# Own semaphores, an early close of the Tile context and one last wait in a split GELU-multiply kernel

## The chip, the cores and the metric

One core of one Trainium2 chip. The metric is the device time of one execution in microseconds (us), as the median over executions. Each listed execution has also a *span*, from the first to the last instruction that the profile records on the core; it is given to 0.1 us. The time is always a little longer than the span, and that difference turns out to matter here, so I call it the *outside*: time minus span of the same execution.

## The reference

```python
def reference(x):                       # x: (32, 512, 2048) float32
    half_dim = x.shape[-1] // 2
    x1, x2 = x[..., :half_dim], x[..., half_dim:]
    gelu_x1 = 0.5 * x1 * (1 + erf(x1 / np.sqrt(2)))
    return (gelu_x1 * x2).astype(np.float32)
```

134 MB are read, 67 MB written, and there are one GELU and one multiply for each output.

## The kernel before

The rows are cut in 16 tiles of 128 partitions x 8 rows. A tile's load is 8.4 MB, its store 4.2 MB. Two buffers hold inputs, two hold outputs. SP issues the loads, ScalarE (ACT) the GELU and most stores, VectorE (DVE) multiplies in place. Tile, a scheduling layer, sets every semaphore (a counter by which one engine or transfer releases another). At the end comes its teardown: it lets SP wait for all transfers, and then puts an all-engine barrier (where each engine waits for all others), a clearing of its semaphores, and a second barrier.

```python
    def load(i):
        x_tile = xpool.tile([P, R, dim], x.dtype, name="x_tile")
        for rows in (slice(0, 4), slice(4, 8)) if i == 0 else (slice(0, 8),):
            dma = nc.sync.dma_start(out=x_tile[:, rows, :], in_=x_t[i][:, rows, :])
            ...
    ahead = [load(0), load(1)]
    for i in range(n_tiles):
        ...
        for lo, hi in steps:            # 2+2+4 rows in the first and last tile, else 5+3
            ...nc.scalar.activation(out=o_tile[:, rows, :], in_=x_tile[:, rows, :half], func=GELU)
            mul = nc.vector.tensor_mul(out=o_tile[:, rows, :], in0=o_tile[:, rows, :], in1=x_tile[:, rows, half:])
            ...
            if pieces and hi % 4 == 0:
                store(nc.sync if last else nc.scalar, i, o_tile, slice(hi - 4, hi))
        ...
        if i + 2 < n_tiles:
            ahead.append(load(i + 2))
...
    with _tile.TileContext(nc) as tc:           # the teardown stands at the end of this block
        tile_split_gelu_mul_kernel(tc, *args)
```

## Time and profile before

| | before |
|---|---|
| time, median | 470.59 us |
| span of the profiled execution | 469.09 us |
| first load issued by SP | 0.730 |
| first GELU starts | 12.906 |
| last multiply ends | 460.839 |
| last store has landed | 468.173 |
| from there to the span's end | 0.917 |

The rows below the second are times in the trace of that one execution, in us from the span's start. The profile's own lines are shown in the prediction, with how each is read.

### The profile page before, as it was taken

Reading aid. Unit: us, or ns where it says so; the run is one execution under the profiler, and the core shown is the slowest. Engines: PE = TensorE matmul, PEld = TensorE weight load, DVE = VectorE, ACT = ScalarE, POOL = GpSimd, SP = SyncE. Lnnn points to the kernel's source line nnn. Section 1 sums busy time; section 2 is a strip of 40 time slices with the busy share of each in tenths; the row PEclk is TensorE's granted clock in tenths of the full one; section 3 lists DMA queues with packets and bytes.
Section 4 is the critical chain, followed back from the end, with each engine's and each line's share of the span. In section 5 each row is a group of like instructions: output and inputs, shape, how many; then the busy total and the mean of one; then the engine's idle time right before and its main releaser. Section 6 shows DMA issues by size and latency. Waiting matters only on the chain.

```text
span 469.1 us, 179 instructions
## 1 busy us (share of the span) xinstructions
DVE 140.5 (30%) x34; ACT 115.5 (25%) x35; POOL 0.2 (0%) x4
## 2 busy tenths in 40 slices
DVE  0330615206051160611506015070250702407042
ACT  1320606041060410605005050050601406014060
POOL 0000000000000000000000000000000000000000
DMA  8999999999999999999999999999999999999998
GB/s 358 447 447 447 414 391 492 402 402 447 492 402 402 447 469 425 402 441 408 492 402 425 425 492 402 402 447 486 408 402 444 455 441 402 441 408 486 408 406 355
DMA packets 5041, 201.34 MB, mean 429 GB/s; under 512 B 560, under 2 KB 560, under 8 KB 560
## 3 DMA queue, kind: packets, MB, share of 16 engines
q1 hardware_dynamic: 2880, 142.61, 70.4%
q10 hardware_dynamic: 2160, 58.72, 29.0%
q14 instruction: 1, 0.01, 0.0%
HBM read 134.22 MB, written 67.11 MB: 429 GB/s over the span
## 4 chain that ended last, share of the span: by engine, by line
DMA 75%; DVE 14%; ACT 8%; ACTq 0%; issue 0%; SPq 0%
DMA out_dram<-o_tile 66%; DVE o_tile L75 14%; DMA x_tile<-in_x_dram 10%; ACT o_tile L71 8%; ACTq L115 0%; SPq L49 0%
## 5 line engine op out<-in xcount | busy, mean ns | idle before, releaser
L75 DVE TENSOR_TENSOR o_tile<-o_tile,x_tile 128x5120 f32<-128x5120 f32 (+3 forms) x34 | 140.5, 4171 | 320.4 <-ACT o_tile L71 320.4
L71 ACT ACTIVATE o_tile<-x_tile 128x5120 f32<-128x5120 f32 (+3 forms) x34 | 114.3, 3407 | 340.1 <-DMA out_dram<-o_tile 302.4
L71 ACT ACT_TABLE_LOAD x1 | 1.3, 1283 | 0.7 <-PEq L104 0.7
L104 POOL MEMSET const-bfloat16-1.0<- 128x1 bf16 x1 | 0.1, 101 | 0.0
L104 POOL MEMSET const-uint8-127<- 128x1 uint8 x1 | 0.1, 101 | 0.0
L104 POOL MEMSET const-float32-0.0<- 128x1 f32 x1 | 0.1, 98 | 0.2 <-issue 0.2
L104 POOL MEMSET const-float32-1.0<- 128x1 f32 x1 | 0.1, 98 | 0.0
## 6 DMA issues: line engine op xcount, KB each, us to landing
out_dram<-o_tile ACTq DMA_DIRECT2D x13, 4096.0 KB, 44.8
x_tile<-in_x_dram SPq DMA_DIRECT2D x2, 4096.0 KB, 16.8
out_dram<-o_tile ACTq DMA_DIRECT2D x2, 2048.0 KB, 34.3
out_dram<-o_tile SPq DMA_DIRECT2D x1, 4096.0 KB, 25.2
out_dram<-o_tile SPq DMA_DIRECT2D x2, 2048.0 KB, 7.5
x_tile<-in_x_dram SPq DMA_DIRECT2D x15, 44.6
```

What stands on the lines that cost most here:

```text
L71: nc.scalar.activation(out=o_tile[:, rows, :], in_=x_tile[:, rows, :half], func=GELU)
L75: mul = nc.vector.tensor_mul(out=o_tile[:, rows, :], in0=o_tile[:, rows, :], in1=x_tile[:, rows, half:],)
L104: nc = _bacc.Bacc("TRN2", target_bir_lowering=False, num_devices=1)
```

## The change

Its intent: get rid of Tile's bookkeeping where it stands on the path. The kernel brings its own semaphores. The Tile context is closed right behind the issue of the first three loads, which stand in a `tile_critical` section ("the section" below), so that its teardown runs while they are on their way. The program ends with one wait for the last stores, and nobody else waits.

```diff
+    first = nc.alloc_semaphore("first")
+    loaded = [nc.alloc_semaphore(f"loaded{k}") for k in range(2)]
+    ...                                   # stored, gelu_done, mul_done, tail_stored
-    ahead = [load(0), load(1)]
+    with tc.tile_critical():
+        load(0, slice(0, 4), first)
+        load(0, slice(4, 8), loaded[0])
+        load(1, slice(0, 8), loaded[1])
+    tc.close()
+    tc.compile()
     for i in range(n_tiles):
+        if i >= 2:
+            nc.scalar.wait_ge(stored[k], n[stored[k].name])
...                                        # a wait ahead of each GELU, multiply and store
         if i + 2 < n_tiles:
-            ahead.append(load(i + 2))
+            nc.sync.wait_ge(mul_done, n[mul_done.name])
+            load(i + 2, slice(0, R), loaded[k])
+    nc.scalar.drain()
+    for sem in (first, *loaded, *stored):
+        nc.scalar.sem_clear(sem)
+    nc.vector.drain()
+    nc.vector.sem_clear(gelu_done)
+    nc.sync.sem_clear(mul_done)
+    nc.sync.wait_ge(tail_stored, n[tail_stored.name]).then_inc(
+        tail_stored, -n[tail_stored.name]
+    )
```

The tiles, the order of work on each engine and the queues are the same, and in both built programs the four buffers lie at the same addresses.

More of the change, by code (lines that the diff above doesn't have):

```diff
@@ L40, with counted, load, store @@
     n_tiles = x_t.shape[0]
-    xpool = ctx.enter_context(tc.tile_pool(name="xpool", bufs=2))
-    opool = ctx.enter_context(tc.tile_pool(name="opool", bufs=1))
-    o_tiles = [opool.tile([P, R, half], out.dtype, name=f"o{k}_tile") for k in range(2)]
-    def load(i):
-        x_tile = xpool.tile([P, R, dim], x.dtype, name="x_tile")
-        for rows in (slice(0, 4), slice(4, 8)) if i == 0 else (slice(0, 8),):
-            dma = nc.sync.dma_start(out=x_tile[:, rows, :], in_=x_t[i][:, rows, :])
-            before_gelu[i % 2].append(dma.ins)
-        return x_tile
-    def store(queue, i, o_tile, rows):
-        dma = queue.dma_start(out=o_t[i][:, rows, :], in_=o_tile[:, rows, :])
-        before_gelu[i % 2].append(dma.ins)
-    before_gelu = [], []
-    ahead = [load(0), load(1)]
+    x_bufs = [nc.alloc_sbuf_tensor(f"x{k}_tile", [P, R, dim], x.dtype) for k in range(2)]
+    o_bufs = [nc.alloc_sbuf_tensor(f"o{k}_tile", [P, R, half], out.dtype) for k in range(2)]
+    first = nc.alloc_semaphore("first")
+    loaded = [nc.alloc_semaphore(f"loaded{k}") for k in range(2)]
+    stored = [nc.alloc_semaphore(f"stored{k}") for k in range(2)]
+    gelu_done = nc.alloc_semaphore("gelu_done")
+    mul_done = nc.alloc_semaphore("mul_done")
+    tail_stored = nc.alloc_semaphore("tail_stored")
+    n = {sem.name: 0 for sem in [first, *loaded, *stored, gelu_done, mul_done, tail_stored]}
+    def counted(ins, sem, by):
+        ins.then_inc(sem, by)
+        n[sem.name] += by
+    def load(i, rows, sem):
+        counted(
+            nc.sync.dma_start(out=x_bufs[i % 2][:, rows, :], in_=x_t[i][:, rows, :]), sem, 16
+        )
+    def store(queue, i, rows, sem):
+        queue.wait_ge(mul_done, n[mul_done.name])
+        counted(
+            queue.dma_start(out=o_t[i][:, rows, :], in_=o_bufs[i % 2][:, rows, :]), sem, 16
+        )
+    with tc.tile_critical():
[4 more added lines that the diff above has]
+    tc.compile()
     for i in range(n_tiles):
-        x_tile = ahead.pop(0)
-        o_tile = o_tiles[i % 2]
+        k = i % 2
         last = i == n_tiles - 1
@@ L66 @@
         steps = ((0, 2), (2, 4), (4, 8)) if pieces else ((0, 5), (5, 8))
-        muls = []
+        if i >= 2:
+            nc.scalar.wait_ge(stored[k], n[stored[k].name])
         for lo, hi in steps:
             rows = slice(lo, hi)
-            tc.keep_in_program_order(
+            if i == 0 and lo == 0:
+                nc.scalar.wait_ge(first, n[first.name])
+            elif lo == 0 or (i == 0 and lo == 4):
+                nc.scalar.wait_ge(loaded[k], n[loaded[k].name])
+            counted(
@@ L71 @@
                 nc.scalar.activation(
-                    out=o_tile[:, rows, :], in_=x_tile[:, rows, :half], func=GELU
-                )
-            )
-            mul = nc.vector.tensor_mul(
-                out=o_tile[:, rows, :],
-                in0=o_tile[:, rows, :],
-                in1=x_tile[:, rows, half:],
-            )
-            for ins in before_gelu[i % 2]:
-                tc.declare_no_dep(mul.ins, ins, reason="ScalarE waited for it")
-            muls.append(mul.ins)
+                    out=o_bufs[k][:, rows, :], in_=x_bufs[k][:, rows, :half], func=GELU
+                ),
@@ L83 @@
+                gelu_done,
+                1,
+            )
+            nc.vector.wait_ge(gelu_done, n[gelu_done.name])
+            counted(
+                nc.vector.tensor_mul(
+                    out=o_bufs[k][:, rows, :],
+                    in0=o_bufs[k][:, rows, :],
+                    in1=x_bufs[k][:, rows, half:],
+                ),
+                mul_done,
+                1,
+            )
             if pieces and hi % 4 == 0:
-                store(nc.sync if last else nc.scalar, i, o_tile, slice(hi - 4, hi))
@@ L85 @@
-        before_gelu[i % 2].extend(muls)
+                if last:
+                    store(nc.sync, i, slice(hi - 4, hi), tail_stored)
+                else:
+                    store(nc.scalar, i, slice(hi - 4, hi), stored[k])
         if not pieces:
-            store(nc.sync if i == n_tiles - 2 else nc.scalar, i, o_tile, slice(0, R))
+            if i == n_tiles - 2:
+                store(nc.sync, i, slice(0, R), tail_stored)
+            else:
+                store(nc.scalar, i, slice(0, R), stored[k])
@@ L88 @@
         if i + 2 < n_tiles:
-            ahead.append(load(i + 2))
+            nc.sync.wait_ge(mul_done, n[mul_done.name])
[8 more added lines that the diff above has]
+        tail_stored, -n[tail_stored.name]
+    )
 _INS = ['x']
```

## The prediction

> **What bounds the kernel now.** I read the page first (engines, queues), then the chain that ended last, then busy time by stretch over single periods of the chain, and last the instructions of the teardown line L115 and who the queues waited for.
>
> ```profile
> span 469.1 us, 179 instructions
> DVE 140.5 (30%) x34; ACT 115.5 (25%) x35; POOL 0.2 (0%) x4
> q1 hardware_dynamic: 2880, 142.61, 70.4%
> q10 hardware_dynamic: 2160, 58.72, 29.0%
> ```
>
> No compute engine is busy for a third of the span, while the two DMA queues together fill 70.4 + 29.0 = 99.4% of the 16 engines' time. That share alone isn't proof of saturation (packets overlap, and the share passes 1.0 in some stretches), so I look at the rate over whole periods. The chain, in order of time:
>
> ```profile
> 0.66 0.07 issue
> 0.73 0.38 SPq L49
> 1.11 0.05 issue
> 1.16 0.42 SPq L49
> 1.59 0.05 issue
> 1.64 45.42 DMA x_tile<-in_x_dram
> ...
> 100.48 4.48 ACT o_tile L71
> 104.96 0.02 issue
> 104.98 8.77 DVE o_tile L75 x2
> 113.75 0.02 issue
> 113.77 44.69 DMA out_dram<-o_tile
> ...
> 456.41 4.43 DVE o_tile L75
> ```
>
> The columns are start, duration and what. The first tiles' load begins at the third issue (1.64), and from then on a period of two tiles repeats: GELU 4.48, multiply 8.77, store 44.7, some 58.0 us. Is it a chain of latencies, or is the store that slow because the DMA engines are full? The rate over single periods (columns: window and length, busy time and count by engine, clock, DMA share, GB/s):
>
> ```profile
> 0.00:1.50 1.50, 0.00 (x0) 0.78 (x1) 0.20 (x4) 1.00 0.00 0
> 100.48:158.49 58.01, 17.52 (x4) 14.25 (x5) 0.00 (x0) 1.00 1.00 434
> 158.49:216.57 58.08, 17.52 (x4) 14.24 (x4) 0.00 (x0) 1.00 1.00 433
> 448.98:467.50 18.52, 8.92 (x3) 7.21 (x3) 0.00 (x0) 1.00 0.95 409
> 467.50:469.09 1.59, 0.00 (x0) 0.00 (x0) 0.00 (x0) 1.00 0.00 0
> ```
>
> 433 to 434 GB/s in each period, whatever the engines do meanwhile: the transfers are the bound, and the 44.7 us of a store are queueing. Only three stretches are not at that rate: the first 1.5 us, the end from 449 on (409), and the last 1.59 us in which nothing moves. A change of synchronization can win only there. The teardown line shows what the last stretch is (columns: count, then minimum/median/maximum ns, first and last start):
>
> ```profile
> L115 SPq EVENT_SEMAPHORE  x6: 17/28/6882, 461.2 to 469.0; - x6
> L115 SPq DRAIN  x3: 7/7/7, 468.4 to 468.7; - x3
> SPq L115 <- DMA out_dram<-o_tile: 6.9, 1, 6.9
> SPq L115 <- PEq L115: 0.6, 2, 0.4
> ```
>
> The long event, 6.882 us, is the wait for the last stores. In the trace's own records it starts at 461.314, so it ends at 468.196; all that stands after it, to 469.09, is 0.89 us: two more semaphore waits, three drains and two all-engine barriers with a clearing of semaphores between them.
>
> **What the Trainium skill says.** "DMA: Bandwidth & Descriptors", section "Where 436 GB/s comes from", puts the ceiling of a core's 16 engines at 435.2 GB/s; the periods' 434 agree, so there is nothing to win in the middle. The same page, "Anatomy of one DMA", says the semaphore of a DMA fires only after its last byte is confirmed, so the last wait costs something beyond the last byte; the trace agrees (nothing moves from 467.5, the wait ends at 468.2), and the new kernel keeps that wait. "Perfetto Trace Analysis", section "Per-instruction lifecycle", says that of a sequencer instruction only its execution is profiled, and the propagation of its semaphore is not; the trace agrees: barrier events are 17 to 51 ns long but stand some 40 to 80 ns apart, so I count them by their distances. "Runtime: NRT & Kernel Launch", section "The launch sequence", names a barrier and semaphore resets that the runtime puts behind a kernel; the trace shows none of it, and the measured time is only 470.59 - 469.09 = 1.5 us above the span.
>
> **The change part by part.**
> Waits in the loop. The order of instructions on each engine is the same in both built programs: 34 multiplies, 35 activations with the table load, the same loads and stores on the same queues. The old program puts a separate semaphore event before most loads, for the landing of the buffer's earlier load; SP spends 214.3 us in those, but each is followed on the same queue by the wait for the multiply, which goes on for 13 us more (182.9 us in 14 waits), so taking them away moves no load. Loads and stores are released by the same multiplies and GELUs by the same landings. Worth: 0.0 us.
>
> Start. In the old program SP's barrier event starts at 0.647 and the first load at 0.730. The new one puts a critical section around the three loads: one more no-op that raises a semaphore, and a second branch that waits for it, ahead of the first load. Neighbouring SP instructions stand 55 to 69 ns apart (the events and drains between 461.2 and 468.4); a semaphore from one engine to another took 42 ns (POOL 0.605 to SP 0.647). Two instructions at some 60 ns and one hop at some 40: +0.16 us, by estimate. It is on the path, as the transfers are the bound from the first packet.
>
> Moved teardown. Behind the third issue (about 2.06) SP leaves the section and goes through the two barriers, 0.7 us in the old tail (468.36 to 469.04), 1 us with the branches and the section's end. It is over near 3.2. ScalarE's table load, 1.28 us, now comes behind it and ends near 4.5; the first GELU waits for its data until 12.91, and SP's fourth load isn't due before the multiply that ends at 30.7. All of it is hidden with over 8 us to spare. Worth: 0.0 us.
>
> End. Behind the last multiply (460.84) SP issues the store, clears one semaphore (93 ns in the old program on GpSimd), and does one wait for 48 counts. The wait is 6.9 us, so the clearing is hidden in it. The other engines' drains and clears come before that wait ends. What stays behind the wait's end at 468.196 is its own record, some 0.02. Saved: 0.89 - 0.02 = 0.87 us.
>
> Sum: +0.16 - 0.87 = -0.71 us on a span of 469.09, thus 468.4; with the same 1.5 us outside the span the time is 469.9 us. I put it at 469.8, as the four other engines being done early may shorten a little of those 1.5 us too.
>
> **The rivals.**
> First, no gain at all: the measured time is taken from marks that the runtime's own closing barrier sets, and its other work waits for the same last store, or the 0.89 us merely come back as the runtime's. For it: 1.5 us of the time are outside the profile. Against it: the removed barriers stand strictly before the program's end, so what follows starts earlier. It would make 470.5 to 470.7.
> Second, a larger gain: the old bookkeeping slows something in the loop, for example the order in which SP's load and ScalarE's store get in when one multiply releases both. Both wait for the same semaphore count before and after, and the periods are already at 434 GB/s. Even the end stretch, 18.5 us at 409, would give only 18.5 x (1 - 409/434) = 1.1 us if all of it came to full rate, and nothing in the change touches it. It would make 468.7.
> Third, a loss: the close is not free of the loads. If the drain at the end of the critical section waited for the loads to land (4, 4 and 8 MB; the third lands at 47.06), the first GELU would wait for the third load instead of the first. No other transfer could be issued before: the DMA engines would run dry from 47.1 until the first store, one GELU (1.9) and two multiplies (2.3 each) later, 6.5 us, and partly again until the fourth load behind the first tile's last multiply: some 8 us lost, 478. Against it: the drains in the trace are 7 to 8 ns on SP, the ScalarE and VectorE drains that do last (7.2 and 4.5 us at the end) wait for their own engine's running instruction, and SP's drain in the built program waits only for SP's own semaphore, none of a load. I give it 2%.
>
> **Range and chances.** The two terms are each known to 0.1 or so, the old runs lie within 470.54 to 470.74, and the packets of the two queues may interleave differently by some tenths. So 469.0 to 470.6. A gain of 2% would be 9.4 us, over three times all the time in which the DMA engines are not at their rate: 0.01. A loss of 2% needs the third rival: 0.01. Within 2%: 0.98.
>
> **What would show it.** Right: the span is 0.7 us shorter; the last record is SP's wait, with no barrier behind it and under 0.1 us after it; the first load issues near 0.89; barrier events and the range clear stand between 2 and 4 us; the first GELU starts at about 13.1, moved by no more than the first load; every period keeps 58.0 us and 433 to 434 GB/s. Wrong: the first load later than 1.2 would mean that the section's entry costs more; a first GELU after 14 means the teardown isn't hidden; a span 0.7 shorter at an unchanged time means the first rival; a period other than 58.0 means that the waits in the loop did matter.

## The result, and the profile after

| | before | after |
|---|---|---|
| time, median of 5 | 470.59 us | 469.56 us |
| lowest and highest | 470.51 to 470.79 | 469.46 to 469.64 |
| span of the profiled execution | 469.09 | 468.14 |
| first load issued | 0.730 | 0.936 |
| first GELU starts | 12.906 | 12.989 |
| last multiply ends | 460.839 | 460.641 |
| last store has landed | 468.173 | 468.102 |
| from there to the span's end | 0.917 | 0.034 |

The ratio is 0.9978 with a 95% interval of 0.9966 to 0.9990: within 2%, and clear of 1. Ratios are the mean time of one kernel's fast runs over that of the other's fast runs of the same rounds, so they are not quite the ratio of the medians quoted.

The chain of waits of the changed kernel, its start (start, duration, what):

```profile
0.67 0.05 issue
0.71 0.01 SPq L58
0.73 0.06 issue
0.78 0.03 SPq L63
0.82 0.12 issue
0.94 0.38 SPq L47
...
1.84 45.44 DMA x_tile<-in_x_dram
```

Ahead of the first load (L47) stand now a no-op (L58) and a branch (L63) that waits for the no-op's semaphore, the entry of the section. Every issue up to the third is 0.206 us later than before, and the long load of the chain starts at 1.84 instead of 1.64.

The moved teardown on SP, and ScalarE's table load behind it (count, minimum/median/maximum ns, first and last start):

```profile
L63 SPq DRAIN  x3: 7/7/7, 2.6 to 2.9; - x3
L63 SPq EVENT_SEMAPHORE  x2: 17/17/17, 2.8 to 3.2; - x2
L79 ACT ACT_TABLE_LOAD  x1: 1283/1283/1283, 3.3 to 3.3; - x1
```

Both barriers are over at 3.2 us, and the first GELU waits for data until 12.99.

The stretches as before, by engine and rate (window and length, busy time and count by engine, clock, DMA share, GB/s), and the last line's instructions on SP with the wait in front of it:

```profile
0.00:1.50 1.50, 0.00 (x0) 0.00 (x0) 0.20 (x4) 1.00 0.00 0
100.68:158.67 57.99, 17.52 (x4) 14.24 (x4) 0.00 (x0) 1.00 1.00 434
158.67:216.68 58.01, 17.52 (x4) 14.24 (x4) 0.00 (x0) 1.00 1.00 434
448.96:467.50 18.54, 8.92 (x3) 7.22 (x3) 0.00 (x0) 1.00 0.98 421
467.50:468.14 0.64, 0.00 (x0) 0.00 (x0) 0.00 (x0) 1.00 0.00 0
```

```profile
L116 SPq EVENT_SEMAPHORE  x1: 17/17/17, 468.1 to 468.1; - x1
SPq L116 <- SPq L116: 7.0, 1, 7.0
```

The wait for the last stores is still 7.0 us long, but 0.034 us behind the last landing the program is over. Where before 1.59 us without data stood behind 467.50, now 0.64 do.

Two things do not add up yet. The two profiled executions differ by 0.95 us in span, but start and end account for 0.883 - 0.206 = 0.68 only. The rest lies in the loop, where the old trace's periods are 58.01 to 58.18 us and the new one's 57.99 to 58.01. And the medians of the listed spans tell another story than these two traces: the kernel before has 468.8 in the later runs (468.7 to 469.1 in 11 executions beside the first experiments), so its profiled execution was one of its longest; the changed kernel has 468.2 (468.1 to 468.3 in the five of this result), and its profiled one is the shortest of five. By the medians the span shrank by 0.6 us, and the time by 1.03. So some 0.4 us of the gain is not in the span at all.

### The profile page after: what moved, and what is told of

It reads as the page before. It is cut to its first block, busy times and chain, and to the rows that moved or that the text cites. A ratio compares the mean times of both kernels' runs of the same rounds, so it can differ in the third digit from the quotient of the medians.

```text
span 468.1 us, 174 instructions
## 1 busy us (share of the span) xinstructions
DVE 140.5 (30%) x34; ACT 115.5 (25%) x35; POOL 0.2 (0%) x4
## 4 chain that ended last, share of the span: by engine, by line
DMA 76%; DVE 14%; ACT 8%; ACTq 0%; SPq 0%; issue 0%
DMA out_dram<-o_tile 66%; DVE o_tile L87 14%; DMA x_tile<-in_x_dram 10%; ACT o_tile L79 8%; ACTq L110 0%; SPq L47 0%; SPq L63 0%; SPq L58 0%
```

## The experiments

Two questions: does the old synchronization cost anything in the loop (theory 2), or are the longer periods chance of the execution (theory 1)? And where is the gain that is not in the span? All kernels here gave correct results. Differences from the changed kernel are between medians; the medians of the kernel before were 470.56 to 470.61 beside all of them, on two chips.

**Both kernels again, as controls.** No edit.

> The kernel before, unchanged, as a control: ratio 1.000, its interval is what these rounds can tell apart. Its trace is a second look at the loop. Theory 1 (the loop's extra 0.4 us between 160 and 410 us in the first trace of before is chance of how packets interleave): the period of two tiles varies by some hundredths of a us between the two traces of before. Theory 2 (the old landing waits cost something in the loop): the last multiply again comes about 0.4 us later, counted from the first load's issue, than in the changed kernel.

> The changed kernel, unchanged, on the same chip as the others: 1.0 us below before (469.5), first load issued at 0.94, nothing behind the last wait. Counted from the first load's issue to the last multiply's end: theory 1 says 459.7 to 460.2, anywhere in the range of before; theory 2 says 459.7, always below before's 460.1.

Measured: before 470.62 us, ratio 1.0007 (0.9994 to 1.0021); after 469.57, ratio 0.9980 (0.9967 to 0.9993). So the gain of 1.0 us comes again. The outside, time minus span of the same execution, is 1.79 us (median of 11) for the kernel before and 1.30 to 1.34 for the changed one: here is the missing 0.4. As to the loop, the second trace of before took 460.00 us from the first load's issue to the last multiply's end (first trace 460.11, changed kernel 459.71), which spoke for theory 2. The changed kernel's trace was of no help for that, as it fell on an execution of 472.57 us that lost some 3 us between 30 and 117 us. One of the six executions of before, 472.86, was as long.

**Two barriers put back at the end.**

```diff
     nc.sync.wait_ge(tail_stored, ...).then_inc(tail_stored, ...)
+    nc.all_engine_barrier()
+    nc.all_engine_barrier()
```

> The changed kernel with two all-engine barriers put back behind its last wait. If the 0.89 us of barriers behind the last wait are worth their length: the records behind the last wait are 0.7 to 0.9 us long again, and the time is 0.7 to 0.9 above the changed kernel, so 0.1 to 0.4 below before (0.2 dearer in the start, so any remaining gain is the loop's). Rival (the runtime's own end hides them): the time stays at 469.5 while the span grows.

Measured: 470.62 us, ratio 1.0000 (0.9988 to 1.0012). The whole gain is gone, 1.05 us, more than expected. The profile shows the first barrier (L119) on SP; the second ends at 468.70:

```profile
L119 SPq DRAIN  x1: 7/7/7, 468.1 to 468.1; - x1
L119 SPq EVENT_SEMAPHORE  x1: 17/17/17, 468.3 to 468.3; - x1
```

From the last landing to the span's end it is 0.683 us, against 0.034: 0.65 in the span. The outside went from 1.3 to 1.79: 0.45 more. The two make 1.1. The rival, that the runtime's end hides such barriers, falls: they cost more than their length.

**No Tile context at all.**

```diff
-    with tc.tile_critical():
-        load(0, slice(0, 4), first)
-        ...
-    tc.close()
-    tc.compile()
+    load(0, slice(0, 4), first)
+    ...
-    with _tile.TileContext(nc) as tc:
-        tile_split_gelu_mul_kernel(tc, *args)
+    tile_split_gelu_mul_kernel(nc, *args)
```

> The changed kernel without any Tile context: no section ahead of the first load, no teardown. The section costs 0.206 us by the two traces: first load at 0.73, time 0.2 below the changed kernel, about 469.3, the best of all. Rival (a later stage absorbs the start): first load at 0.73 and the time at 469.5.

Measured: 469.36 us, the lowest median of all, 0.21 below the changed kernel on the same chip; ratio to before 0.9983 (0.9967 to 0.9998), whose mean holds one execution of 471.9. The start of its chain is the old one:

```profile
0.73 0.38 SPq L46
...
1.63 45.43 DMA x_tile<-in_x_dram
```

The section's 0.2 us at the start are thus paid in full, and can be had back.

**The context closed ahead of the loads.**

```diff
-    with tc.tile_critical():
-        load(0, slice(0, 4), first)
-        ...
     tc.close()
     tc.compile()
+    load(0, slice(0, 4), first)
+    ...
```

> The changed kernel with the context closed ahead of the three loads instead of behind them: the teardown's two barriers, some 0.9 us with branches, stand ahead of the first load, so it issues at 1.6 to 1.8 instead of 0.94. If the transfers are the bound from the first packet, time and span grow by the same 0.7 to 0.9: 470.3 to 470.5. Rival (slack behind the first load absorbs a later start): 469.6.

Measured: 470.00 us. I had taken the teardown for longer than it is where nobody is late: it sets the first load back by 0.65 us against the bare kernel, from 0.733 to 1.381, and so by 0.445 against the changed kernel. Its chain of waits has the first load at:

```profile
1.38 0.38 SPq L47
```

The time is 0.43 above the changed kernel's 469.57 (measured on the other chip, where the kernel before took 470.59 against 470.56 here). With the run before it: a start that is 0.20 earlier gives 0.21, one that is 0.44 later costs 0.43. The start counts one to one, and the rival, slack behind the first load, falls.

**The landing waits put back in the loop.**

```diff
         if i + 2 < n_tiles:
+            if i == 0:
+                nc.sync.wait_ge(first, n[first.name])
+            nc.sync.wait_ge(loaded[k], n[loaded[k].name])
             nc.sync.wait_ge(mul_done, n[mul_done.name])
```

> The changed kernel with the old kernel's second wait put back on SP in front of each load, for the landing of the buffer's earlier load, which is long over. Theory 1 (the loop's synchronization moves nothing; the traces' 0.4 us are chance): 469.5 to 469.7, span 468.2, as the changed kernel; each later load issues at most one instruction, 0.07 us, behind its multiply's release. Theory 2 (such waits cost in the loop): 469.9 to 470.0, span 468.6.

Measured: 469.62 us, span 468.3, as the changed kernel within the noise. In the built program the wait for the multiply came to stand in the separate event and the landing on the load itself, so each later load is issued behind ScalarE's store by 0.04 us instead of just ahead of it. Even that did nothing to the periods:

```profile
114.20:172.18 57.99, 17.52 (x4) 14.24 (x4) 0.00 (x0) 1.00 1.00 434
172.18:230.19 58.01, 17.52 (x4) 14.25 (x4) 0.00 (x0) 1.00 1.00 434
```

**A third trace of the kernel before.** No edit.

> The kernel before once more, for a third trace. Its first two traces have spans of 469.09 and 468.97 and periods of 58.02 to 58.18 us, where traces of kernels with own semaphores have 58.00; but the median span of the kernel before over 31 listed executions is 468.8. Theory 1 (chance of the execution): a trace with a span near 468.75 has periods nearer 58.00, and from the first load's issue to the last multiply's end it takes some 459.8, as the changed kernel. Theory 2 (the old waits): periods of 58.04 or more and 460.0 again, whatever the span.

Measured: 472.78 and 470.52 us. The profiled execution was the long one, so the test by its span could not be made: it lost 2.3 us before 116 us. But its later periods can be read, and so can those of the changed kernel's disturbed trace. First the kernel before, then the changed kernel:

```profile
174.13:232.12 57.99, 17.52 (x4) 14.25 (x4) 0.00 (x0) 1.00 1.00 434
232.12:290.13 58.01, 17.52 (x4) 14.25 (x4) 0.00 (x0) 1.00 1.00 434
```

```profile
175.10:233.16 58.06, 17.52 (x4) 14.25 (x4) 0.00 (x0) 1.00 1.00 432
233.16:291.21 58.05, 17.52 (x4) 14.25 (x4) 0.00 (x0) 1.00 1.00 432
```

The old synchronization ran periods of 58.00, and the new one ran 58.06. Both rhythms occur in both kernels, so they belong to the execution and not to the waits. With the waits put back at no cost, theory 2 falls.

**All engines wait at the end, without a barrier.**

```diff
     nc.sync.wait_ge(tail_stored, ...).then_inc(tail_stored, ...)
+    nc.sync.nop().then_inc(ended, 4)
+    for e in (nc.gpsimd, nc.scalar, nc.vector, nc.tensor):   # written out
+        e.wait_ge(ended, 1).then_inc(ended, -1)
```

> The changed kernel, whose four other engines now also wait at the very end, for a count that SP gives behind its last wait; no barrier. In the first four runs the span and the time were listed together: before lies 1.8 us above its span, the changed kernel 1.34, the one with two barriers put back 1.8. Theory A (0.4 us of the gain is outside the span: engines that end early do their part of what closes the program while the last store is still under way): span 468.3, time 1.7 to 1.8 above it, 470.0 to 470.1. Theory B (only barriers as such cost that): span 468.3, time 1.35 above it, 469.65.

Measured: 470.18 us, of which 468.4 are span and 1.80 outside. The span grew by 0.155 (last landing to its end 0.189), the outside by 0.46. Theory B falls: to keep the other four engines until the end costs 0.46 us beyond the last instruction, without any barrier.

**The last wait on another engine.** Which engine is it?

```diff
-    nc.sync.wait_ge(tail_stored, n[tail_stored.name]).then_inc(
+    nc.gpsimd.wait_ge(tail_stored, n[tail_stored.name]).then_inc(   # or scalar, vector, tensor
```

> The changed kernel with its last wait on GpSimd instead of SP, which then ends at 461. What stands outside the span was 1.34 us where SP alone ends last and 1.80 where all five end together, so some engine other than SP has 1.80 us of its own behind its last instruction. If it is GpSimd: time minus span 1.75 to 1.8, time 470.0. If not: 1.34 or less, 469.55 or less.

> The same with the last wait on ScalarE. If ScalarE is the engine with 1.80 us behind its last instruction: time minus span 1.75 to 1.8, time 470.0. If not: 1.34 or less.

> The same with the last wait on VectorE. If VectorE is the engine with 1.80 us behind its last instruction: time minus span 1.75 to 1.8, time 470.0. If not: 1.34 or less.

> The same with the last wait on TensorE. If TensorE is the engine with 1.80 us behind its last instruction: time minus span 1.75 to 1.8, time 470.0. If not: 1.34 or less; if it is 1.34 on all engines, theory A holds only for several ending together, by contention in what closes the program.

Measured (median time and outside; the last two columns are explained below and come from the profiled execution):

| last wait on | time | outside | last instruction to sign-off | sign-off to end of the pass |
|---|---|---|---|---|
| SP (the changed kernel) | 469.56 | 1.34 | 0.14 | 0.16 |
| VectorE | 469.67 | 1.43 | 0.19 | 0.24 |
| ScalarE | 469.74 | 1.47 | 0.15 | 0.33 |
| TensorE | 469.96 | 1.65 | 0.28 | 0.36 |
| GpSimd | 470.10 | 1.90 | 0.56 | 0.29 |

The last instruction in the GpSimd version is as short as on SP and comes at the same moment:

```profile
L116 POOLq EVENT_SEMAPHORE  x1: 17/17/17, 468.1 to 468.1; - x1
```

I had expected one engine at 1.8 and the others at 1.34 or less. In fact each has its own distance from its last instruction to the end of the measured time, GpSimd's the longest and SP's the shortest. (The spans are given to 0.1 us, so the 0.09 between SP and VectorE is near what these medians can tell apart.)

The traces hold the reason, though no view of the profile prints it: they also keep the moments at which semaphores change, beyond the last instruction too. Semaphore 2, which no instruction in the traces names, changes nine times behind the kernel (the *pass*), over 200 others change next, and then it changes nine times more. In all 13 traces whose execution has a listed time, the last of these changes lies 0.11 to 0.13 us above that time, so the outside is this closing. In the pass, the change that comes late is the first where TensorE has the last wait, the second for ScalarE, the third for GpSimd, the fourth for VectorE and the fifth for SP. Read so, the engines sign off one behind the other in that order, and four more changes follow.

An engine that ends early has signed off early: in the changed kernel's trace the first four stand at 3.49, 456.69, 456.73 and 460.94. So much of theory A holds, and no more: the other semaphores change only from 0.11 us before the end of the pass on, in every trace. What differs are the last two columns of the table; from the end of the pass to the last change it is 1.14 to 1.15 us in all five.

With that the kernel before adds up. In its trace GpSimd's last instruction ends at 469.00, 0.09 before the span's end, which TensorE's longer event sets. But GpSimd's sign-off comes 0.56 us later, at 469.56, and 0.205 behind ScalarE's, where the same step takes 0.04 when GpSimd is early: the pass waited for GpSimd. The pass is over 0.76 us behind the span's end, in the version with two barriers 0.76 too, and 0.30 in the changed kernel's trace: the difference is the missing 0.45. So in the old kernel GpSimd, whose only work is four small fills at the start, set the end of the measured time, and in the new one SP does.

## Why the prediction was right or wrong

The time, 469.56 us, lies inside the range, and the direction and the place of the gain were right. The predicted gain was 0.8 us (0.71 from the sum), the measured one 1.03. By its steps:

- *Loop, 0.0.* Right. The waits put back cost nothing. The prediction's own warning sign, "a period other than 58.0", did show between the first two traces, and was misleading: both rhythms appear in both kernels. One thing about its source: the section that it cites for 435.2 GB/s also says that transfers between HBM and SBUF are bound lower, at some 358 GB/s. The 434 GB/s of these periods are above that, and the measurement decides.
- *Start, +0.16.* Right in mechanism, a bit small: 0.206. The branch and its waits took longer than two common instructions: 0.12 us alone stand between the branch and the load. One to one on the path, as the bare kernel and the early close show.
- *Moved teardown, 0.0.* Right: over at 3.2 as said, the table load at 4.6, the first GELU at 12.99.
- *End, -0.87.* Right: 0.883 (0.917 to 0.034).
- *Outside the span, "may shorten a little of those 1.5 us too".* This is the term that was mis-sized. I took 0.1 for it; it was 0.45. The first cause is arithmetic: the 1.5 came from a median time less the span of another, long execution. Pairs of the same execution give 1.79. The second is that I thought of the closing as one thing behind the last instruction. It is a pass in which each engine signs off in its turn, and a sign-off that comes early costs nothing. GpSimd, which the old kernel keeps to the end, takes 0.56 us to sign off, SP 0.14, and two steps fewer are left behind SP's. Why GpSimd takes so long, no run here shows. The prediction's remark on the runtime's barrier and semaphore resets, "the trace shows none of it", holds for the views only: the semaphore changes behind the last instruction fit both.
- *First rival, no gain because the runtime's closing takes it back.* It was wrong in sign: the closing gave 0.45 more. *Third rival, a teardown that waits for the loads.* Did not occur: SP's drain at the section's end took 55 ns.
- *The chances.* 9.4 us are "over three times" the idle time only if the stretch from 449 on is left out: 1.5 + 1.59 = 3.1 us, and 4.2 with the 1.1 us that the prediction itself gives that stretch. Nothing hangs on it.

The sum with measured terms: +0.206 - 0.883 - 0.45 = -1.13 against -1.03 measured. The remaining 0.1 is no more than what undisturbed executions of one kernel differ by (469.46 to 469.64, 470.51 to 470.79).

Open stays what happens in the executions that are 2 to 3 us longer. They occur in both kernels (472.57, 472.86, 472.78) and in the bare one (471.9); where a trace fell on one, the time was lost in transfers before 117 us, at full clock.

## What to carry to other kernels

Where transfers fill the whole span, synchronization is worth something only before the first transfer and behind the last one, and there it counts one to one: issue the first load ahead of any bookkeeping, and let bookkeeping run under the loads. At the end, let the engines that have nothing more to do finish early and keep only one short wait, on the engine that is quickest from its last instruction to the end of the measured time (here SP); a closing barrier costs its own length and also what the slowest engine (here GpSimd) still takes to sign off. Compare a time only with the span of the same execution, and look at several executions before reading a few tenths of a microsecond out of two traces.

## What the Trainium skill lacked or had wrong

- "Runtime: NRT & Kernel Launch", section "The ~15µs preamble/postamble breakdown", lists what follows a kernel as stages with one time each. It lacks that the part behind the last instruction depends on the engine that ends last (outside 1.34 us for SP, 1.43 for VectorE, 1.47 for ScalarE, 1.65 for TensorE, 1.90 for GpSimd), the order in which the engines sign off there, and that GpSimd takes 0.56 us to do so where the others take 0.14 to 0.28.
- "Perfetto Trace Analysis", section "Per-instruction lifecycle", says that the semaphore wait of a sequencer-only instruction is not in its profiled time. That holds for the changed kernel's last wait (17 ns for a wait of 7.0 us), but the old kernel's event with two semaphores was recorded with 6,882 ns, the wait for the last stores included. The prediction's remark that the trace agrees is right only for the short barrier events.
- No page has the executions that are 2 to 3 us longer at full clock (469.6 against 472.6 for the same kernel), with the loss in the first quarter of the transfers.
